# A stage of DeltaNet heads whose order is set by a clock that follows every emitted instruction

## The chip, the cores and the metric

The kernel runs on one core of one Trainium2 chip. The metric is the device time of one execution in microseconds (us); the time before is the median of three runs. Its engines are PE (TensorE, matmul), DVE (VectorE), ACT (ScalarE), POOL (GpSimd) and SP (SyncE, which issues the DMAs here). Each engine executes its own instructions in the order in which the program gives them, and waits at an instruction until the semaphores that it needs have come.

## The reference

One layer of a bidirectional encoder on 1024 tokens and 16 meta tokens, width 1024, float32:

```python
h = rmsnorm(h_res, norm1_w[l])
proj = h @ w_in[l]
(q, k, v, z, b_raw, a_raw, sc_b, sc_c, sc_x, gate_a, gate_b) = jnp.split(proj, SPLIT_POINTS, axis=-1)
o_dn = gated_deltanet_bidir(q, k, v, z, b_raw, a_raw, dn_conv_w[l], A_log[l], dt_bias[l], dn_norm_w[l])
y_a = o_dn @ w_branch_dn[l]
y_b = (sc_b * depthwise_conv_centred(sc_c * sc_x, sc_conv_w[l])) @ w_branch_sc[l]
merged = jax.nn.sigmoid(gate_a) * y_a + jax.nn.sigmoid(gate_b) * y_b
h_res = h_res + merged @ w_out[l]
h2 = rmsnorm(h_res, norm2_w[l])
gu = h2 @ w_gate_up[l]
h_res = h_res + (jax.nn.silu(gu[..., :D_FF]) * gu[..., D_FF:]) @ w_down[l]
```

The DeltaNet has 8 heads of width 128. For each head, q, k and v go through a convolution over five tokens and SiLU; then a gated delta rule runs over chunks of tokens, forwards and backwards. A chunk needs products of keys with keys and of queries with keys times a decay (an exponential of differences of cumulated gates), the inverse of a triangular matrix, and a recurrence with a 128 x 128 state S:

```python
v_new = u_c - jnp.einsum("bhcd,bhde->bhce", w_c, S)
o_c = (jnp.einsum("bhcd,bhde->bhce", qd_c, S)
       + jnp.einsum("bhij,bhje->bhie", qk_c, v_new))
S = S * gl_c[..., None, None] + jnp.einsum("bhcd,bhce->bhde", kd_c, v_new)
```

## The kernel before

Every large product is made of three fp32r matmuls: both operands are split into a high part (a cast on ACT) and a low part (a subtraction on DVE), and high x high, high x low and low x high are summed in a PSUM bank.

The kernel has three stages. In the first 75 us the input is normed, scaled and transposed, and the first units start. In the *stage of heads*, up to about 905 us, PE does two things at once. The *dense units* (`u_qkv`, `u_short`, `u_z`) multiply the whole sequence by 128 columns of `w_in`: the matmuls of L335, in two or three chunks of 320 to 512 tokens with eight steps of three matmuls each. Between two steps the kernel emits what the *streams* have ready. For each head these are: `g_decay` (fetches rows of cumulated gates from DRAM into `PQ`, L507, adds a mask on DVE, L511, and takes the exponential on ACT, L530), `g_norm` (transposes, norms, then for eight chunks the product `kkq` of keys with keys and queries, L587, which DVE multiplies into `NP`, L619, and `PQ`, L625), `g_meta`, `g_inv` (the inverse of eight blocks, with a long chain of small DVE steps in `fs_job`, L477 and L481), `g_vals`, `g_scan` (the recurrence) and `g_out`. The convolutions (L361, with SiLU on ACT at L365) and other chains of DVE are *jobs* in lanes, which `pump` emits where DVE has room. Behind the stage follow the branches, the merge and the feed-forward part, up to 2009 us.

A scan step (`g_scan`) does two directions at a time: S times keys (L807) and queries (L810), r on DVE (L817), `NP` x r (L822), w and v on ACT (L829, L834), keys x w (L839), `PQ` x v (L842), the new S on DVE (L852), and the outputs o (L870, L873, L876).

What is emitted when is planned by the program as it builds the instructions. `T` holds a time for each engine. `pe(ns)` adds to PE's, `on(e, ns)` to another engine's, with flat prices that stand beside each instruction or group; a generator yields the time from which its next step may be emitted, and `run_streams` goes on with it when PE's time has come there. The margins are flat: 200 ns behind PE, 370 behind the others, and 5000 for the decay rows from DRAM:

```python
HOP, TOPE, DEP = 200, 370, 127
ARRIVE = 5000
def on(e, ns, ready=0.0):
    T[e] = max(T[e], ready, T["pe"]) + ns
    return T[e] + TOPE
```

A weight (128 columns) is loaded two units ahead (`pick`), and split in four parts by `split_part`: casts on ACT (L958) and subtractions on DVE (L955), at steps 4, 6, 8 and 10 of the unit before (`SPL`). PSUM has eight banks: three for dense units (`pm`), two for `pe` (transposes, `kkq`), two for `pd` (the scan) and one, `pv`, that values, inverse and outputs share by a lock.

Of the kernel before, what the change touches and what calls it, by code (L numbers as in the profile page):

```python
# [8 lines left out]
F32 = mybir.dt.float32  # L9
# [7 lines left out]
P = 128  # L17
# [17 lines left out]

@with_exitstack
def encoder_layer(ctx: ExitStack, tc: tile.TileContext, x, meta, norm1_w, w_in,
                  dn_conv_w, A_log, dt_bias, dn_norm_w, sc_conv_w, w_bdn, w_bsc,
                  w_out, norm2_w, w_gu, w_down, final_w, out):
    nc = tc.nc  # L40
# [29 lines left out]
    def psv():  # L70
        return ps.tile([P, 512], F32, tag="v", name=uid("pv"), bufs=1)

    rot = {"i": 0}
# [6 lines left out]
    make_identity(nc, ident)  # L80
# [133 lines left out]
    HOP, TOPE, DEP = 200, 370, 127  # L214
    ARRIVE = 5000
    LOAD = 1283
    LAND = 5500
    T = {"pe": 0.0, "dve": 0.0, "act": 0.0, "pool": 0.0}

    def on(e, ns, ready=0.0):  # L220

        T[e] = max(T[e], ready, T["pe"]) + ns
        return T[e] + TOPE

    def pe(ns):
        T["pe"] += ns
        return T["pe"] + HOP

    def V(n, kind=0):
        return on("dve", (68 + 1.042 * n, 130 + 1.042 * n, 130 + 0.52 * n)[kind])  # L230

    def A(n):
        return on("act", 144 + 0.834 * n)
# [40 lines left out]
    def block_sums():  # L274
# [13 lines left out]
        for name, t, terms in (  # L288
# [4 lines left out]
            for k in (slice(0, 2), slice(2, 4)):  # L293
                x0 = terms[0]
                x0 = x0[0](x0[1], k, x0[2]) if isinstance(x0, tuple) else x0[:, k]
                for op, *y in terms[1:]:
                    y = y[0](y[1], k, y[2]) if len(y) == 3 else y[0][:, k]
                    nc.vector.tensor_tensor(out=t[:, k], in0=x0, in1=y, op=op)
                    V(1024)
# [27 lines left out]
    def dense_steps(po, w, xx, t0, n, sweep=False):  # L327
# [6 lines left out]
        for i, (k, j) in enumerate(order):  # L334
            mm(po[:, :n], (wl if j == 2 else wh)[:, k], xl[k][:, t0:t0 + n] if j == 1 else xh[k][:, t0:t0 + n],  # L335
               start=(i == 0), stop=(i == 3 * KT - 1))
            if i % 3 == 2:
                pe(3 * (n / 2.4 + 13))
                yield

# [13 lines left out]
    def conv_job(raw, dst, col, st_, first):  # L354

        for h0, hn in ((first, 520 - first), HALF[1]):
            acc = dst[:, h0:h0 + hn]
            while st_["rows"] < h0 + hn + 4:
                yield max(T["pe"], T["dve"]) + 300
            for t in (0, 1, 3, 4):  # L360
                nc.vector.scalar_tensor_tensor(out=acc, in0=raw[:, h0 + t:h0 + t + hn], scalar=wc[:, t, col:col + 1],  # L361
                                               in1=acc, op0=ALU.mult, op1=ALU.add)
                V(hn, 1)
                yield T["dve"] + DEP
            nc.scalar.activation(acc, acc, AF.Silu)  # L365
            on("act", 0, T["dve"] + HOP)
            t = A(hn)
        yield t

    def u_qkv(h, i, w):  # L370
# [5 lines left out]
        for ci, (t0, n) in enumerate(QUERY if i == 1 else QCH):  # L376
# [14 lines left out]
            nc.scalar.copy(raw[:, 2 + t0:2 + t0 + n], po[:, :n])  # L391
            nc.scalar.activation(dst[:, t0:t0 + n], po[:, :n], AF.Copy, scale=wc[:, 2, col:col + 1])  # L392
            A(n)
            A(n)
            sub["rows"] = 2 + t0 + n if ci < 2 else L + 4
# [9 lines left out]
    def short_job(cx, j, ycs):  # L405
        for i in range(2):
# [3 lines left out]
            yield A(512)  # L410
            for t in range(1, 3):
# [3 lines left out]
                V(512, 1)  # L415
# [3 lines left out]
    def u_short(j, i, w):  # L419
        st_ = shorts[j]  # L420
        if i < 2:
            for t0, n in ((14, 322), (336, 320), (656, 384)):
# [7 lines left out]
                if i == 0:  # L430
                    nc.scalar.copy(sl, po[:, :n])
                    A(n)
                else:
                    nc.vector.tensor_tensor(out=sl, in0=po[:, :n], in1=sl, op=ALU.mult)
                    V(n)
            if i == 1:
                st_["yc"] = []
# [4 lines left out]
        else:  # L442
            force(shorts[-1]["job"])
# [56 lines left out]
    def g_decay(h, st_):  # L500
# [14 lines left out]
        for i0, i1 in ((0, 6), (6, 8)) if h > 1 else ((0, 8),):  # L515
            for i in range(i0, i1):
# [3 lines left out]
                if i - 2 >= i0:  # L520
                    masked(i - 2)
# [1462 lines left out]
```

## Time and profile before

| | |
|---|---|
| runs | 2008.42, 2010.34, 2012.87 us; median 2010.34 |
| profiled execution | 2011.13 us; its span, first to last instruction, 2009.4 us |
| mean granted clock of PE | 0.992 |
| instructions | 32113; matmuls 11914 |
| table loads of ACT | 26, of 1283 ns each |

In the views, a row of a list of instructions gives line, engine, operation, written and read tiles, shape and count; then busy time in us, the mean length in ns, and the idle time of the engine just before, with its releaser. A row of the timeline begins with the start and the length in us (one length for a merged row, "x2"), and gives an idle time before it in brackets. A row of the waits gives who waited for whom, the total in us, how often, and the longest. A row of the windows gives the length of the stretch, then the busy time of each engine with its count of instructions, the granted clock of PE (1.00 is full), the busy share of the DMA engines and GB/s. Small matmuls in full float32 show as two records each.

### The profile page before, as it was taken

What the parts mean: (1) busy time and instruction counts of PE and PEld (TensorE: products, weight loads), DVE (VectorE), ACT (ScalarE), POOL (GpSimd) and SP (SyncE); (2) the same over time, 40 slices, a digit from 0 to 9 for tenths busy, and PEclk for the clock granted to TensorE, in tenths of its full rate; (3) what the DMA queues carried; (4) which work ended last, traced back from release to release, by engine and by line L of the source; (5) the groups of instructions that cost most, each with busy time, mean ns of one, the idle gap of its engine ahead of it and who ended that gap; (6) DMA issues with size and microseconds to landing.
All of it is one profiled execution on the core that took longest, in us unless ns stands there. A gap on an engine that the chain in (4) does not pass through costs nothing.

```text
span 2009.4 us, 32113 instructions
## 1 busy us (share of the span) xinstructions
PE 1951.0 (97%) x11914; PEld 1707.5 (85%) x11914; DVE 1423.4 (71%) x2733; ACT 984.2 (49%) x2198; POOL 164.7 (8%) x497
## 2 busy tenths in 40 slices
PE   9999999899999999999999999999999999999998
PEld 8987889899889989988887788888888888888887
DVE  4757577688768777772666897748887877756574
ACT  5664576767666764631444545224322322225343
POOL 2113200202111120000000000000000000000001
PEclk9999999999999999999999999999999999999999
DMA  4222212122121211244899732322576655487654
GB/s 142 66 59 85 74 49 59 40 60 59 38 60 40 62 46 53 75 159 135 326 307 319 271 128 74 126 92 74 188 241 211 215 168 173 158 283 245 194 177 159
DMA packets 221681, 275.76 MB, mean 137 GB/s; under 512 B 15140, under 2 KB 134341, under 8 KB 220117
## 3 DMA queue, kind: packets, MB, share of 16 engines
q1 hardware_dynamic: 221525, 273.72, 41.8%
q8 instruction: 93, 1.52, 0.3%
q14 instruction: 63, 0.52, 0.1%
HBM read 197.03 MB, written 76.63 MB: 136 GB/s over the span
## 4 chain that ended last, share of the span: by engine, by line
PE 79%; DVE 8%; ACT 7%; DMA 4%; issue 2%; SPq 0%; POOL 0%; POOLq 0%; DVEq 0%; ACTq 0%
PE pm L335 24%; PE pm L1413 4%; PE pm L1710 3%; PE pe L1413 3%; PE pm L1711 3%; PE pm L1709 2%; PE pd L1413 2%; PE pe L1710 2%; PE pd L1710 2%; PE pe L1711 2%; PE pe L1709 2%; PE pd L1709 2%; PE pd L1711 2%; PE pm L1868 1%; PE pm L1867 1%
## 5 line engine op out<-in xcount | busy, mean ns | idle before, releaser
L335 PE MATMUL pm<-hTh,wh 128*128 128x384 f32 (+4 forms) x1200 | 434.2, 363 | 2.1 <-ACT kq L392 1.2
L335 PE MATMUL pm<-al,wh 128*128 128x384 f32 (+4 forms) x1200 | 402.4, 336 | 0.5 <-DVE al L1075 0.5
L335 PE MATMUL pm<-hTh,wl 128*128 128x384 f32 (+4 forms) x1200 | 402.6, 336 | 0.0
L335 PEld LDWEIGHTS pm<-hTh,wh 128*128 128x128 f32 x1200 | 228.0, 190 | 13.2 <-ACT kq L392 1.6
L335 PEld LDWEIGHTS pm<-al,wh 128*128 128x128 f32 x1200 | 228.3, 190 | 9.6 <-DVE al L1075 0.7
L335 PEld LDWEIGHTS pm<-hTh,wl 128*128 128x128 f32 x1200 | 227.3, 190 | 10.2
L89 DVE TENSOR_TENSOR al<-raw,ring_h 128x1024 fp32r<-128x1024 f32 x73 | 88.5, 1222 | 65.2 <-ACT ring_h L88 64.8
L88 ACT CAST ring_h<-raw 128x1024 fp32r<-128x1024 f32 x73 | 76.9, 1055 | 110.9 <-PE pv L1868 37.5
L955 DVE TENSOR_TENSOR wl<-raw,wh 128x512 fp32r<-128x512 f32 x108 | 74.0, 686 | 77.8 <-ACT wh L958 77.6
L361 DVE SCALAR_TENSOR_TENSOR kq<-ra,wc,kq 128x520 f32<-128x520 f32 (+1 forms) x128 | 95.7, 748 | 14.4 <-ACT kq L392 13.0
L88 ACT CAST raw<-pair 128x1024 fp32r<-128x1024 f32 (+1 forms) x56 | 53.8, 961 | 94.9 <-PE pe L1413 31.6
L130 POOL TENSOR_SCALAR ss<-ss 128x1 f32<-128x1 f32 x13 | 4.6, 350 | 1061.1 <-ACT b L1878 602.6
L88 ACT CAST wh<-pair 128x1024 fp32r<-128x1024 f32 (+1 forms) x56 | 53.8, 960 | 59.7 <-PE pv L1413 29.8
L89 DVE TENSOR_TENSOR raw<-pair,raw 128x1024 fp32r<-128x1024 f32 (+1 forms) x56 | 61.9, 1104 | 27.6 <-ACT raw L88 27.5
L89 DVE TENSOR_TENSOR wl<-pair,wh 128x1024 fp32r<-128x1024 f32 (+1 forms) x56 | 61.9, 1105 | 25.1 <-ACT wh L88 25.1
L958 ACT CAST wh<-raw 128x512 fp32r<-128x512 f32 x108 | 66.4, 619 | 23.5 <-PE pm L335 23.3
L829 ACT ACTIVATE w<-pd,small 128x128 f32<-128x128 f32 x128 | 39.9, 364 | 74.2 <-PE pd L822 64.0
L481 DVE TENSOR_TENSOR fP<-fP,tm 128x126 f32<-128x126 f32 (+22 forms) x248 | 62.7, 253 | 6.4
L477 DVE TENSOR_TENSOR tm<-fP,fN 128x126 f32<-128x126 f32 (+22 forms) x248 | 62.6, 253 | 6.2
L132 POOL TENSOR_TENSOR small<-small,minus_half 128x9 f32<-128x9 f32 x16 | 30.6, 1910 | 406.0 <-DVE small L592 255.7
L587 PE MATMUL pe<-kq 128*128 128x256 f32 x128 | 38.7, 403 | 24.3 <-DVE PQ L625 15.1
L1368 DVE TENSOR_TENSOR b<-pm,b 128x512 f32<-128x512 f32 x65 | 43.6, 684 | 24.6 <-PE pm L1711 22.2
(729 smaller groups left out, 5228.5 us busy)
## 6 DMA issues: line engine op xcount, KB each, us to landing
raw<-in_w_in_dram SPq DMA_DIRECT2D x56, 512.0 KB, 4.3
raw<-in_w_gate_up_dram SPq DMA_DIRECT2D x44, 512.0 KB, 5.2
sums<-in_w_down_dram SPq DMA_DIRECT2D x22, 512.0 KB, 4.8
t_d<-sums SPq DMA_DIRECT2D x11, 1024.0 KB, 3.9
raw<-s_d SPq DMA_DIRECT2D x44, 256.0 KB, 3.4
raw<-t_d SPq DMA_DIRECT2D x44, 256.0 KB, 3.7
act_d<-b SPq DMA_DIRECT2D x43, 256.0 KB, 2.7
pair<-in_w_in_dram SPq DMA_DIRECT2D x10, 1024.0 KB, 10.3
```

The source lines that it names most:

```text
L88: nc.scalar.copy(hi, src)
L89: nc.vector.tensor_tensor(out=lo, in0=src, in1=hi.bitcast(F32), op=ALU.subtract)
L335: mm(po[:, :n], (wl if j == 2 else wh)[:, k], xl[k][:, t0:t0 + n] if j == 1 else xh[k][:, t0:t0 + n], start=(i == 0), stop=(i == 3 * KT - 1))
L361: nc.vector.scalar_tensor_tensor(out=acc, in0=raw[:, h0 + t:h0 + t + hn], scalar=wc[:, t, col:col + 1], in1=acc, op0=ALU.mult, op1=ALU.add)
L477: nc.vector.tensor_tensor(out=tv, in0=fP[:, 0:r, j:j + 1].broadcast_to([P, r, n]), in1=fN[:, j:j + 1, j + 1:32].broadcast_to([P, r, n]), o ...
L481: nc.vector.tensor_tensor(out=fP[:, 0:r, j + 1:32], in0=fP[:, 0:r, j + 1:32], in1=tv, op=ALU.subtract)
L955: nc.vector.tensor_tensor(out=u[1][1][:, k], in0=u[2][:, k], in1=u[1][0][:, k].bitcast(F32), op=ALU.subtract)
L958: nc.scalar.copy(u[1][0][:, k], u[2][:, k])
L1413: mm(bank[t], a[:, c], b, start=fresh, stop=first and k == 3 and j == 2, skip_group_check=not first)
L1709: mm(po, ah[:, k], bhk, start=k == 0, stop=False)
L1710: mm(po, ah[:, k], blk, start=False, stop=False)
L1711: mm(po, al[:, k], bhk, start=False, stop=k == 3)
```

## The change

Arithmetic, tiles and instructions stay; 10304 matmuls, 2733 DVE, 1942 ACT, 497 POOL instructions and 852 DMAs are there in both, up to the bank of one tile. Only their order in the stage of heads is another. The change puts a `Clock` behind every call of an engine: it computes when the instruction can start from its own engine's time and from what wrote or read its operands, and takes its price from its kind and size. `V()`, `A()` and `pe()` now only read when the last instruction of that engine ends, plus 25 or 45 ns; `after(x)` says when a tile is ready.

Further: evictions of dense banks are emitted when the clock has the matmuls done (`later`), not right behind them. The exponentials come in groups of six with room between, and a SiLU of a convolution waits until a group is over. A part of a weight is split only once the clock has its input there and the engine free. `kkq` puts two products in one bank and runs up to three ahead. The tile `E` of the inverse lies in `pv` rather than `pm`. In the scan the products with queries come behind L822, both w and v are waited for, and the two additions of an output pair stand together.

```diff
+class Clock:
...
+    def known(self, ap, write=False, e=None):
+        key, p0, p1, lo, hi = self.region(ap)
+        t = self.free.get(key, 0.0) if write else 0.0
+        for r in self.seen[key]:
+            if r[0] < p1 and p0 < r[1] and r[2] < hi and lo < r[3]:
+                t = max(t, 0.0 if e == "pe" == r[6] else r[4], r[5] if write or ap.space == PSUM and e != r[6] else 0.0)
+        return t
...
+    def cost(self, e, op, outs, ins, args):
...
+            if ins[0].dtype == F32R:
+                return m / 2.4 + 14.5, m / 2.4 + 190
...
+            return max(224, m / 0.6 + 9), 212 + max(m, 72) / 0.75
+        if e == "act":
+            t = 150 + 0.79 * n if not psum else 145 + 0.65 * n
...
+    def did(self, e, op, a, kw):
...
+        ready = max([self.known(x, False, e) for x in ins] + [self.known(x, True, e) for x in outs])
+        if e == "sp":
+            start = max(self.T[e], ready + 26)
+            self.T[e] = start + 430
...
+            land = max(start + 1500, self.ring) + n / (20 if run < 64 else 230 if run < 1024 else 330)
+            self.ring = land
+            end = land + 200
+        else:
+            occupied, took = self.cost(e, op, outs, ins, kw)
...
+            start = max(self.T[e], ready + (45 if e == "pe" else 80 if e == "pool" else 34))
...
+    HOP, DEP = 150, 127
+    T = clock.T
+    def on(e):
+        return clock.end[e] + 45
+    def pe():
+        return clock.end["pe"] + 25
+    def after(*aps):
+        return max(clock.known(x) for x in aps) + 45
...
+    def run_late(flush=False):
+        while late and (flush or late[0][0] <= T["pe"]):
+            late.pop(0)[1]()
...
+            while lock["exp"]:
+                yield max(T["pe"], T["dve"]) + 200
             nc.scalar.activation(acc, acc, AF.Silu)
...
-                arrived.append(fetch(i))
-                if i - 2 >= i0:
-                    masked(i - 2)
-            for i in (i1 - 2, i1 - 1):
-                yield arrived[i]
+                yield clock.known(PQ[:, i], True)
+                fetch(i)
+            for i in range(i0, i1):
+                yield after(PQ[:, i])
                 masked(i)
...
+            lock["exp"] = True
...
+                if i % 3 == 2:
+                    yield T["act"] - 300
+            lock["exp"] = False
...
         def kkq(c):
-            pk = psd()
+            if not banks:
+                bank = psd()
+                banks.extend((bank[:, :2 * P], bank[:, 2 * P:]))
+            pk = banks.pop(0)
...
-        E = psm().rearrange("p (d c i) -> p d c i", d=2, c=NC)
+        yield from take("inv")
+        E = psv().rearrange("p (d c i) -> p d c i", d=2, c=NC)
...
-    def split_part(u, i):
+    def split_part(u, i, must=True):
+        k = slice(4 * (i // 2), 4 * (i // 2) + 4)
+        if not must and clock.known(u[1][0][:, k] if i % 2 else u[2]) > max(T["pe"], T[("act", "dve")[i % 2]]):
+            return
...
-            if ahead[0] and n_ in SPL:
-                split_part(ahead[0], SPL.index(n_))
+            run_late()
+            if ahead[0] and n_ >= SPL and ahead[0][3][0] < 4 and n_ % 2 == 0:
+                split_part(ahead[0], ahead[0][3][0], False)
             run_streams()
             pump()
```

Since every call goes through one wrapper, all rows of the changed kernel have its line, L187. Three places show the new order. On ACT, around the first exponentials of the fourth head (`PQ_695`; `wh` is the high part of the next weight, w and v belong to the scan of the second head before it, `ra` and `vT` are evictions), before:

```order
L530 ACT_TABLE_LOAD
L530 ACTIVATE PQ_695<-PQ_695,negG_681 128x128 x12
L958 CAST wh_4314<-raw_4057 128x512
L829 ACTIVATE w_4406<-pd_4373,small_1782 128x128
L829 ACTIVATE w_4408<-pd_4373,small_1782 128x128
L834 ACTIVATE v_673_4410<-pd_4373,small_1782 128x128
L834 ACTIVATE v_674_4412<-pd_4373,small_1782 128x128
L391 COPY ra_4417<-pm_4318 128x336
L392 ACTIVATE vT_3461<-pm_4318,wc 128x336
L958 CAST wh_4314<-raw_4057 128x512
```

And in the changed kernel, at the same exponentials:

```order
L187 CAST wh_3971<-raw_3698 128x512
L187 ACT_TABLE_LOAD
L187 ACTIVATE PQ_695<-PQ_695,negG_681 128x128 x6
L187 ACTIVATE w_4028<-pd_3981,small_1691 128x128
L187 ACTIVATE w_4030<-pd_3981,small_1691 128x128
L187 ACTIVATE v_588_4032<-pd_3981,small_1691 128x128
L187 ACTIVATE v_589_4034<-pd_3981,small_1691 128x128
L187 COPY ra_4042<-pm_3975 128x322
L187 CAST wh_3971<-raw_3698 128x512
L187 ACTIVATE PQ_695<-PQ_695,negG_681 128x128 x6
```

The twelve exponentials have become two sixes, the scan's w and v and the second cast stand between them, and the first cast stands ahead of the table load.

On DVE, at the same place (`wl` is the low part of the weight, which needs the cast; `fP` and `tm` are the inverse of the head before; `NP` is the first product behind `kkq`), before:

```order
L955 TENSOR_TENSOR wl_4315<-raw_4057,wh_4314 128x512
L477 TENSOR_TENSOR tm_4400<-fP_3675,fN_3674 128x70
L481 TENSOR_TENSOR fP_3675<-fP_3675,tm_4400 128x14x5
L477 TENSOR_TENSOR tm_4414<-fP_3675,fN_3674 128x56
L481 TENSOR_TENSOR fP_3675<-fP_3675,tm_4414 128x14x4
L477 TENSOR_TENSOR tm_4427<-fP_3675,fN_3674 128x45
L481 TENSOR_TENSOR fP_3675<-fP_3675,tm_4427 128x15x3
L477 TENSOR_TENSOR tm_4436<-fP_3675,fN_3674 128x30
L955 TENSOR_TENSOR wl_4315<-raw_4057,wh_4314 128x512
L619 SCALAR_TENSOR_TENSOR NP_693<-pe_4379,small_3921,PQ_695 128x128 x2
```

And in the changed kernel, from the masks of the same rows of decay on:

```order
L187 TENSOR_TENSOR PQ_695<-PQ_695,mask_696 128x256 x5
L187 SCALAR_TENSOR_TENSOR r_583_3994<-pd_3981,negEG,vS 128x128
L187 SCALAR_TENSOR_TENSOR r_584_3996<-pd_3981,negEG,vS 128x128
L187 TENSOR_TENSOR PQ_695<-PQ_695,mask_696 128x256
L187 SCALAR_TENSOR_TENSOR kq_3535<-ra_3774,wc,kq_3535 128x520
L187 TENSOR_TENSOR wl_3972<-raw_3698,wh_3971 128x512
L187 SCALAR_TENSOR_TENSOR kq_3535<-ra_3774,wc,kq_3535 128x520
L187 TENSOR_TENSOR fP_3554<-fP_3554,tm_3950 128x5x23
```

The subtraction now stands behind the cast's new place rather than behind all exponentials, the masks are added together and the last one right behind its landing by the clock, and the chain of the inverse is at an earlier point (5x23 against 14x5).

On PE, in the first scan step of the third head, from keys x w to the next S (`w,kn` and `v,PQ` are L839 and L842; `pm` are dense matmuls; `S,kq` is L807), before:

```order
L839 MATMUL pd_4957<-w_4980,kn_2338 128x128
L839 MATMUL pd_4957<-w_4982,kn_2338 128x128
L842 MATMUL pd_4958<-v_744_4984,PQ_694 128x128
L842 MATMUL pd_4958<-v_745_4986,PQ_694 128x128
L335 MATMUL pm_4991<-hTh_137,wh_4613 128x384
L335 MATMUL pm_4991<-al_134,wh_4613 128x384
L335 MATMUL pm_4991<-hTh_137,wl_4614 128x384
L335 MATMUL pm_4991<-hTh_137,wh_4613 128x384
L335 MATMUL pm_4991<-al_134,wh_4613 128x384
L335 MATMUL pm_4991<-hTh_137,wl_4614 128x384
L807 MATMUL pd_5032<-S_5018,kq_1346 128x128
```

And in the changed kernel:

```order
L187 MATMUL pd_4756<-w_4795,kn_2225 128x128
L187 MATMUL pd_4756<-w_4797,kn_2225 128x128
L187 MATMUL pd_4792<-v_714_4799,PQ_694 128x128
L187 MATMUL pd_4792<-v_715_4801,PQ_694 128x128
L187 MATMUL pm_4812<-hTh_137,wh_4427 128x336
L187 MATMUL pm_4812<-al_134,wh_4427 128x336
L187 MATMUL pm_4812<-hTh_137,wl_4428 128x336
L187 MATMUL pd_4835<-S_4825,kq_1384 128x128
```

Three dense matmuls stand between the step's products and the next S where six stood. Over all 56 steps with a next S, the order has six or more dense matmuls there in 54 before and in 7 now; 34 steps have three, and 15 none, with two to four small matmuls in their place.

More of the change, by code (lines that the diff above doesn't have):

```diff
@@ new lines, with __init__, __getattr__, call @@
+class Engine:
+    def __init__(self, engine, name, clock):
+        self.engine, self.name, self.clock = engine, name, clock
+    def __getattr__(self, op):
+        f = getattr(self.engine, op)
+        def call(*a, **kw):
+            r = f(*a, **kw)
+            self.clock.did(self.name, op, a, kw)
+            return r
+        return call
+class Engines:
+    def __init__(self, nc, clock):
+        for field, name in (("tensor", "pe"), ("vector", "dve"), ("scalar", "act"), ("gpsimd", "pool"), ("sync", "sp")):
+            setattr(self, field, Engine(getattr(nc, field), name, clock))
@@ L39, in encoder_layer @@
                   w_out, norm2_w, w_gu, w_down, final_w, out):
-    nc = tc.nc
+    clock = Clock()
+    nc = Engines(tc.nc, clock)
     x, out = x[0], out[0]
@@ L337, in dense_steps, with later @@
             if i % 3 == 2:
-                pe(3 * (n / 2.4 + 13))
+                pe()
                 yield
+    late = []
+    def later(t, f):
+        late.append((t, f))
+        if not rot["later"]:
+            run_late(True)
+    def run_late(flush=False):
+        while late and (flush or late[0][0] <= T["pe"]):
+            late.pop(0)[1]()
     raws = []
@@ L359, in conv_job @@
                 yield max(T["pe"], T["dve"]) + 300
+            yield after(raw[:, h0:h0 + hn + 4], acc)
             for t in (0, 1, 3, 4):
@@ L498, in take @@
         lock["scan"] = who
+        if lock["bank"] is not None:
+            yield clock.known(lock["bank"], True, "pe") + 45
     def g_decay(h, st_):
@@ L605, in g_norm @@
         PQf = PQ.rearrange("p s d t -> p (s d) t")
-        yield T["act"] + HOP - 300
         order = (3, 4, 2, 5, 1, 6, 0, 7)
         ready = lambda c: (c, 0) in st_["exp"] and (c, 1) in st_["exp"]
-        nxt = None
+        ahead_ = []
         for n, c in enumerate(order):
-            while not ready(c):
-                yield T["pe"] + 200
-            pk, t = nxt or kkq(c)
-            nxt = None
-            if n + 1 < NC and ready(order[n + 1]):
-                nxt = kkq(order[n + 1])
-            yield max(t, st_["exp"][c, 0], st_["exp"][c, 1])
+            for c_ in order[n + len(ahead_):n + 3]:
+                while not ready(c_) and not ahead_:
+                    yield T["pe"] + 100
+                if not ready(c_):
+                    break
+                if not banks:
+                    yield after(cc)
+                ahead_.append(kkq(c_))
+            pk, t = ahead_.pop(0)
+            yield max(t, st_["exp"][c, 0], st_["exp"][c, 1], after(cc))
             for d in range(2):
@@ L703, in g_inv @@
         nc.scalar.mul(T2, pt, -1.0)
[L704 removed]
+        yield max(A(), after(W, XT))
         pp, px = (b()[:, :256].rearrange("p (c i) -> p c i", c=NC) for b in (psv, psm))
```

387 lines of the change are left out of this document (237 added, 150 removed).

## The prediction

> **What bounds the kernel now.** I read the page first, then the windows by stage, the list of waits of each engine, and the timeline around the longest waits.
>
> ```profile
> span 2009.4 us, 32113 instructions
> PE 1951.0 (97%) x11914; PEld 1707.5 (85%) x11914; DVE 1423.4 (71%) x2733; ACT 984.2 (49%) x2198; POOL 164.7 (8%) x497
> PE 79%; DVE 8%; ACT 7%; DMA 4%; issue 2%; SPq 0%; POOL 0%; POOLq 0%; DVEq 0%; ACTq 0%
> ```
>
> TensorE (PE) is busy for 97% of the span, and it is 79% of the chain that ended last. Its work does not change: the change issues the same instructions on each engine. So a gain can only be time in which PE waits, or runs below its clock. The order of the two kernels is the same at the start and again in the long feed-forward part, so the second question is how much of this lies in the stage of heads, which runs from about 75 us to 905 us.
>
> ```profile
> core 0: us, PE busy (x) PEld busy (x) DVE busy (x) ACT busy (x) POOL busy (x), PEclk, DMA share, GB/s
> 75.00:905.00 830.00, 790.85 (x6605) 742.09 (x6605) 605.35 (x1668) 530.61 (x1578) 128.97 (x409) 0.98 0.22 65
> 905.00:2009.40 1104.40, 1091.40 (x4862) 901.20 (x4860) 776.98 (x978) 413.47 (x538) 16.43 (x34) 1.00 0.57 194
> ```
>
> PE idles 830.0 - 790.9 = 39.2 us in the stage of heads, and its granted clock there is 0.98, not 1.00. VectorE (DVE) is 73% busy and ScalarE (ACT) 64%: neither is full. These are the waits of PE in that window (total, times, longest):
>
> ```profile
> PE pe L587 <- DVE PQ L625: 15.1, 9, 2.9
> PE pe L587 <- DVE fP L481: 9.2, 3, 3.6
> PE pd L822 <- DVE r L817: 4.6, 2, 2.7
> PE pd L807 <- DVE S L852: 1.4, 2, 0.7
> PE pd L839 <- ACT v L834: 1.4, 3, 0.6
> ```
>
> L587 is the product of keys with keys and queries; it waits for one of two PSUM banks, which DVE frees with L625. Its two rows are 24.3 us, well over half of the idle time. Why is DVE late? The wait list of DVE and the timeline of the longest case say it:
>
> ```profile
> DVE wl L955 <- ACT wh L958: 69.0, 29, 10.9
> ```
>
> ```profile
> 355.20 1.28 ACT L530 ACT_TABLE_LOAD   x1
> 356.49 3.62 ACT L530 ACTIVATE PQ<-PQ,negG 128x128 f32<-128x128 f32 x12
> 360.02 0.60 ACT L958 CAST wh<-raw 128x512 fp32r<-128x512 f32 x1
> 360.66 0.69 DVE L955 TENSOR_TENSOR wl<-raw,wh 128x512 fp32r<-128x512 f32 x1 [4.66 <-ACT wh L958]
> 364.38 0.41 DVE L625 TENSOR_TENSOR PQ<-pe,PQ 128x256 f32<-128x256 f32 x1
> 364.94 0.87 PE L587 MATMUL pe<-kq 128*128 128x256 f32 x2 [3.63 <-DVE fP L481]
> 365.93 0.53 PE L335 MATMUL pm<-al,wh 128*128 128x384 f32 x1
> ```
>
> The cast L958, the first half of splitting a weight, stands on ACT behind a table load and twelve exponentials. The second half L955 was put on DVE at a fixed step, so DVE, which is in order, stands still for 4.66 us with everything behind it, L625 too, and PE then waits 3.63 us. The last row shows the second price: the dense matmul is on the array for 0.53 us, and this window shows why:
>
> ```profile
> 365.00:370.00 5.00, 4.57 (x18) 4.14 (x18) 4.45 (x14) 1.38 (x7) 2.73 (x11) 0.66 0.08 19
> ```
>
> The granted clock is 0.66 in the 5 us behind the wait. The Trainium skill, page "TensorE: Matmul & The Clock Gate", section "Why this matters for your kernels", says that the array keeps its full rate if no gap between bursts is over about 3 us. The trace agrees for this gap of 3.63 us, and no sum below goes by it.
>
> **The change part by part.** The sum is made against the profiled execution: 2011.13 us, of which 2009.4 are the span. The median of the runs is 2010.34, 0.8 lower.
>
> *Weights split on landing, exponentials in sixes, the clock.* In the first fence of order the cast L958 has moved ahead of the exponentials or between the two sixes, and on DVE (second fence) its partner is emitted only when the clock has the cast done. So the chain "table load, twelve exponentials, cast, subtraction, product" no longer holds DVE. The new product code also puts two products in a bank, so four may be outstanding where two were. Of the 24.3 us I count 20 as gone; at worst, with only the longest cases cured, 12.
>
> *The clock of the array.* 0.02 x 830 = 16.6 us of clock were not granted (12.5 to 20.8 by the rounding of 0.98), some of it while PE was idle anyway. Half-rate stretches follow long waits, so they go with them: 11, between 5 and 17.
>
> *The other visible waits.* 39.2 - 24.3 = 14.9 us lie in many short waits of the scan, the inverse and the weights. The clock prices each hand-over where the old one used a flat 200 or 370 ns. I count half of them, 8 (4 to 13).
>
> *Waits that no idle time shows.* In this stretch a dense matmul takes 0.32 us, but the next starts 0.15 later, so a wait under about 0.16 us is not seen as idle.
>
> ```profile
> 500.90 0.32 PE L335 MATMUL pm<-al,wh 128*128 128x322 f32 x1
> 501.05 0.31 PE L335 MATMUL pm<-hTh,wl 128*128 128x322 f32 x1
> 501.20 0.60 PE L839 MATMUL pd<-w,kn 128*128 128x128 f32 x4
> 501.65 0.61 PE L842 MATMUL pd<-v,PQ 128*128 128x128 f32 x4
> 501.92 0.60 DVE L852 SCALAR_TENSOR_TENSOR S<-S,eGl,pd 128x128 f32<-128x128 f32 x2 [0.43 <-PE pd L839]
> 502.01 0.39 PE L335 MATMUL pm<-hTh,wh 128*128 128x322 f32 x1
> ```
>
> PE has some 400 rows in the stage that wait for DVE or ACT, so the ceiling is 64 us and the floor 0. The visible waits of the scan rows above are few, so I stay near the floor: 10 (0 to 30). Sum of the gains: 20 + 11 + 8 + 10 = 49.
>
> *What it costs: the state's hand-over.* Each of 56 scan steps hands the state S from PE to DVE and back. By the rows above S needs 502.52 - 501.20 = 1.32 us from the first L839. In that time PE has L839 and L842 (0.81 us, from 501.20 to 502.01) and then dense matmuls at 0.15. Before, six to nine stood there in nearly all steps (third fence): 1.7 to 2.2 us, a cushion. Now, by the order, 34 steps have three (1.26), 15 have only two to four small matmuls (taken as two thirds of three dense ones: 0.81 + 0.30 = 1.11), 7 have six or more. With DVE free the shortfall is 34 x 0.06 + 15 x 0.21 = 5 us; a DVE instruction that stands ahead of S now adds its time to PE, and behind the waiting matmul all dense work is queued. I take 6, between 2 and 17 (56 x 0.30, half of the L852 row).
>
> *The masks.* The decay rows come from DRAM, and DVE adds the mask when they have landed. The old code allowed 5000 ns; the new clock computes 1500 + 285 + 200 + 45 = 2030 ns from the issue.
>
> ```profile
> PQ<-grow SPq DMA_DIRECT2D x128, 64.0 KB, 3.0
> DMA to landing us min/median/max: 2.8/3.0/4.6
> DVE PQ L511 <- DMA PQ<-grow: 1.6, 3, 0.6
> ```
>
> The landing takes 3.0 us at the median and never under 2.8, so each last mask can hold DVE for about 1.0 us: 6 heads x 3 masks that are put down right after their landing = 18 us of DVE against 1.6 now. Behind them stand convolution steps with slack, and sometimes S or r. I take a fifth on the path, 4 (0 to 18).
>
> *Table loads.* Sixes with other work between them raise the loads, as the order of ACT lists them, from 26 to 32.
>
> ```profile
> L530 ACT ACT_TABLE_LOAD x9 | 11.5, 1283 | 0.2
> L530 ACT ACTIVATE PQ<-PQ,negG 128x128 f32<-128x128 f32 x128 | 39.0, 388 | 0.1
> ```
>
> 6 x 1.283 = 7.7 us of ACT, covered by its 299 idle us in the stage; on the path they would cost 7.7. I take 0. The Trainium skill, page "ScalarE: Activation LUTs", section "What ACT_TABLE_LOAD costs", says that a drain of about 1.38 us goes with each switch; by it the six would be an estimated 16 us. The trace disagrees: the exponentials start at 356.49, right behind a load of 1.28 that began at 355.20.
>
> *Late evictions*, the order within the scan (second products after L822, additions in pairs) and the other bank for the inverse move instructions and add none; their worth is in the terms above, their price 0, since DVE and ACT are off the path by the window's shares. One doubt stays: the clock prices an exponential at 251 ns, the trace at (3.62 - 0.39) / 11 = 294. It runs early by that much, and so I left part of each gain uncounted.
>
> Sum: 49 - 6 - 4 = 39. 2011.1 - 39 = 1972; as a median, 1971.
>
> **The rivals.**
>
> *It all goes.* Then 24.3 + 16.6 + 14.9 + 16 of hidden waits come back less 4 of hand-over: 68, so 1942 by the median. For it: there is dense work to put in every gap, and DVE is idle for 225 us of the stage. Against it: the clock is 17% short for an exponential and about 1 us for a landing, so some waits stay.
>
> *The wait only moves.* In the bursts ACT itself may be the bound:
>
> ```profile
> 545.00:550.00 5.00, 2.67 (x19) 2.41 (x17) 2.52 (x9) 4.86 (x14) 0.95 (x3) 0.96 0.00 0
> 560.00:565.00 5.00, 5.00 (x121) 4.60 (x120) 2.58 (x5) 4.89 (x15) 2.67 (x11) 1.00 0.01 3
> ```
>
> ACT is 97% busy here, and none of its work goes away. Then PE would wait at the scan or the inverse for what it no longer waits for at L587, and only a fourth of the 49 comes: 12, so 1998. Against it: the second row shows a full ACT beside a full PE, and over the whole stage ACT is 64% busy.
>
> *Slower: no cushion at the hand-overs.* The new clock hands work over with 25 to 45 ns to spare, where the old one kept 200 to 370. If DVE is really later than the clock has it (masks, cheaper prices), PE stalls at every S and every r (56 + 64 = 120 hand-overs in the scan), with no other matmul allowed past. It breaks even at 49 / 120 = 0.41 us each, more than one L852; at 0.6 us it costs 72 - 49 = 23 us: 2033. For it: the masks' 1.0 us. Against it: most hand-overs have nothing long ahead of them in the new order of DVE, and a stall gives DVE time to catch up.
>
> *No change.* That the change does not do what it says is ruled out by the order, in the three fences. Terms that cancel to within 0.2% (4 us, about what a measurement of this kernel can tell from none) are left.
>
> **How the numbers follow.** Forecast (a gain of 20 to 60): 0.60, 1971 us. It all goes: 0.13, 1942. The wait only moves: 0.12, 1998. Slower: 0.10, 2033. Within 4 us: 0.05. With all terms at their worst the gains are 12 + 5 + 4 + 0 = 21 and the costs 17 + 18 = 35, a loss of 14; at their best 24 + 17 + 13 + 30 = 84 less 2, a gain of 82. I leave out half of the first rival and most of the last two: 1944 to 2004. Faster 0.60 + 0.13 + 0.12 = 0.85, less 0.01 for the thin end of the moved wait: 0.84; same 0.05; slower 0.11.
>
> **What would show it right or wrong.** Right: in the stage of heads the idle time of PE falls from 39 us to 10 to 20, and the stage ends near 866 us; the products wait under 6 us in total; DVE's wait for the cast falls from 69 us to under 25; the granted clock is 0.99 or 1.00; the part behind the stage keeps its 1104 us. The masks' wait for the DMA should rise from 1.6 us to 8 or more, and S at the scan should be the largest wait of PE that is left. Wrong: idle time of PE over 30 us, wherever its releaser now is; or a stage that is no shorter though the idle time has gone, which would mean short waits at the hand-overs, to be seen as wider starts of the scan's matmuls; or a later stage that grew.

## The result and the profile after

The changed kernel takes 1984.55 us (median of 4 runs, 1983.66 to 1988.73) against 2011.38 for the kernel before (4 runs): a ratio of 0.9873, 95% interval [0.9854, 0.9891]. About 27 us came where 39 were forecast. Its profiled execution took 1984.57 us. The page, and the windows by stage with the later boundary moved to the new end of the stage of heads:

```profile
span 1982.9 us, 32162 instructions
PE 1949.6 (98%) x11914; PEld 1697.7 (86%) x11914; DVE 1413.5 (71%) x2733; ACT 989.4 (50%) x2204; POOL 168.4 (8%) x497
PE 83%; DVE 8%; DMA 4%; issue 1%; ACT 1%; POOL 1%; SPq 0%; POOLq 0%; DVEq 0%; ACTq 0%
```

```profile
75.00:878.00 803.00, 789.86 (x6610) 732.39 (x6611) 595.87 (x1669) 539.34 (x1595) 133.48 (x409) 1.00 0.23 67
878.00:1982.90 1104.90, 1091.83 (x4862) 902.18 (x4860) 776.97 (x978) 410.06 (x528) 15.62 (x33) 1.00 0.58 193
```

The whole gain is in the stage of heads: it ends at 878 instead of 905, and what follows takes 1104.9 us against 1104.4. PE's idle time there went from 39.2 to 803.00 - 789.86 = 13.1 us, and the granted clock from 0.98 to 1.00. One thing does not fit: idle time fell by 26 and the clock should have given back some 10 more, yet the stage is 27 shorter. PE's busy time, 789.86 against 790.85, should have fallen with the clock and did not. The waits of PE in the stage (who waited for whom, total, times, longest):

```profile
PE pe L187 <- DVE Nm L187: 7.0, 4, 4.6
PE pe L187 <- issue: 2.9, 1, 2.9
PE pm L187 <- ACT kq L187: 1.9, 1, 1.9
PE pe L187 <- DVE PQ L187: 1.4, 5, 0.4
PE pd L187 <- DVE S L187: 0.6, 2, 0.4
```

The two rows of the products, 24.3 us before, are 1.4 (`PQ`). The largest wait is one that nothing in the forecast spoke of: `Nm`, 4.6 us of it in one piece. The timeline shows that place:

```profile
146.18 0.18 POOL L187 TENSOR_TENSOR meta_inv<-meta_inv,tm 16x1 f32<-16x1 f32 x1
146.30 0.17 POOL L187 MEMSET small<- 128x99 f32 x1
146.50 0.27 ACT L187 ACTIVATE jk<-pe 16x128 f32<-16x128 f32 x1 [4.91 <-POOL small L187]
146.90 0.16 DVE L187 TENSOR_TENSOR Nm<-pe,Dm 16x16 f32<-16x16 f32 x1 [4.58 <-ACT jk L187]
147.11 1.11 PE L187 MATMUL pe<-ident,kq 128*128 128x128 f32 x4 [4.64 <-DVE Nm L187]
```

ACT, DVE and PE all stand for 4.6 to 4.9 us behind a memset of 0.17 us, because on POOL that memset was queued behind the chain of small steps of `g_meta`. A half-rate stretch of PE follows: the granted clock is 0.51 from 146.8 to 150.3.

Where the rest went shows in the waits of the *weight loads* (PEld). A matmul's own row hides a wait that the matmul before it covers; the load before it shows it. The three rows of the scan on r, v and S, before:

```profile
PEld pd L822 <- DVE r L817: 5.3, 2, 3.2
PEld pd L839 <- ACT v L834: 3.8, 11, 0.9
PEld pd L807 <- DVE S L852: 1.9, 2, 1.0
```

and after:

```profile
PEld pd L187 <- ACT v L187: 6.2, 22, 0.7
PEld pd L187 <- DVE r L187: 3.7, 10, 0.8
PEld pd L187 <- DVE S L187: 3.5, 12, 0.7
```

A few long waits have become many short ones: 15 with 11.0 us before, 44 with 13.4 us after. One of them in the timeline:

```profile
688.25 0.61 ACT L187 ACTIVATE v<-pd,small 128x128 f32<-128x128 f32 x2
688.50 0.31 PE L187 MATMUL pm<-hTh,wl 128*128 128x320 f32 x1
688.91 0.52 PEld L187 LDWEIGHTS pd<-w,kn 128*128 128x128 f32 x4 [0.36 <-ACT v L187]
688.91 0.71 PE L187 MATMUL pd<-w,kn 128*128 128x128 f32 x4
```

The dense matmul at 688.50 leaves the next start free 0.15 us later, at 688.65. The load waits until 688.91, by its releaser for ACT's v, and PE's row has no bracket: 0.26 us are lost with no idle time shown.

To size it I compared starts: for each matmul in the stage, the time since the start of the one before, less the lower quartile of the same succession of three shapes in the whole trace of before. Summed over the stage, in us (number of places in brackets; places outside the half-rate stretches but for the first and last row):

| excess of a start | before | after |
|---|---|---|
| over 0.6 us, everywhere | 41.5 (26) | 10.9 (7) |
| 0.05 to 0.6 us | 18.9 (166) | 33.7 (279) |
| under 0.05 us | 21.8 | 24.5 |
| half-rate stretches, without waits over 0.6 | 14.0 | 3.1 |

The difference is 30.6 + 10.9 - 14.8 - 2.7 = 24 us of the stage's 27. So the long waits and the clock did come back, 41.5 us of them, and 17.5 went into short waits. The second row depends on the choice of the quartile's sample: with other choices it rises by 10 to 15 us. Two thirds of its rise lie in three groups of the scan: the starts of keys x w, S x keys and `NP` x r hold 16.5 us at 136 places after, 6.8 at 53 before.

### The profile page after: what moved, and what is told of

It reads as the page before. It is cut to its first block, busy times and chain, and to the rows that moved or that the text cites. A ratio compares the mean times of both kernels' runs of the same rounds, so it can differ in the third digit from the quotient of the medians.

```text
span 1982.9 us, 32162 instructions
## 1 busy us (share of the span) xinstructions
PE 1949.6 (98%) x11914; PEld 1697.7 (86%) x11914; DVE 1413.5 (71%) x2733; ACT 989.4 (50%) x2204; POOL 168.4 (8%) x497
## 4 chain that ended last, share of the span: by engine, by line
PE 83%; DVE 8%; DMA 4%; issue 1%; ACT 1%; POOL 1%; SPq 0%; POOLq 0%; DVEq 0%; ACTq 0%
PE pm L187 45%; PE pd L187 18%; PE pe L187 13%; PE pv L187 8%; DMA o_d<-w 1%; DMA w<-o_d 1%; DVE kq L187 1%; DMA PQ<-grow 1%; DVE NP L187 1%; DVE PQ L187 1%; DVE wl L187 1%; DMA pair<-p_d 1%; DVE pair L187 1%; DVE al L187 1%; DVE vT L187 0%
## 5 line engine op out<-in xcount | busy, mean ns | idle before, releaser
L187 PE MATMUL pm<-hTh,wh 128*128 128x384 f32 (+4 forms) x1234 | 442.1, 359 | 1.9 <-ACT kq L187 1.9
L187 PE MATMUL pm<-al,wh 128*128 128x384 f32 (+4 forms) x1234 | 414.0, 336 | 0.5 <-DVE al L187 0.5
L187 PE MATMUL pm<-hTh,wl 128*128 128x384 f32 (+4 forms) x1234 | 413.4, 336 | 0.0
L187 PEld LDWEIGHTS pm<-hTh,wh 128*128 128x128 f32 x1234 | 233.5, 189 | 13.8 <-ACT kq L187 2.1
L187 PEld LDWEIGHTS pm<-al,wh 128*128 128x128 f32 x1234 | 233.6, 189 | 10.8 <-DVE al L187 0.7
L187 PEld LDWEIGHTS pm<-hTh,wl 128*128 128x128 f32 x1234 | 232.2, 188 | 11.1
L187 DVE TENSOR_TENSOR al<-raw,ring_h 128x1024 fp32r<-128x1024 f32 x73 | 88.4, 1223 | 63.8 <-ACT ring_h L187 63.3
L187 ACT CAST ring_h<-raw 128x1024 fp32r<-128x1024 f32 x73 | 76.9, 1054 | 110.1 <-PE pv L187 33.8
L187 ACT CAST wh<-raw 128x512 fp32r<-128x512 f32 (+1 forms) x134 | 93.6, 703 | 74.1 <-PE pm L187 36.1
L187 DVE TENSOR_TENSOR wl<-raw,wh 128x512 fp32r<-128x512 f32 (+1 forms) x132 | 102.9, 780 | 33.6 <-ACT wh L187 33.1
L187 ACT CAST raw<-pair 128x1024 fp32r<-128x1024 f32 (+1 forms) x56 | 53.8, 961 | 94.4 <-PE pe L187 31.6
L187 DVE SCALAR_TENSOR_TENSOR kq<-ra,wc,kq 128x520 f32<-128x520 f32 (+1 forms) x128 | 95.9, 750 | 3.3 <-ACT kq L187 1.8
L187 POOL TENSOR_SCALAR ss<-ss 128x1 f32<-128x1 f32 x13 | 4.6, 352 | 1072.8 <-ACT b L187 602.8
L187 ACT CAST wh<-pair 128x1024 fp32r<-128x1024 f32 (+1 forms) x56 | 53.8, 960 | 59.5 <-PE pv L187 29.8
L187 DVE TENSOR_TENSOR raw<-pair,raw 128x1024 fp32r<-128x1024 f32 (+1 forms) x56 | 61.9, 1106 | 29.0 <-ACT raw L187 28.9
L187 DVE TENSOR_TENSOR wl<-pair,wh 128x1024 fp32r<-128x1024 f32 (+1 forms) x56 | 62.0, 1107 | 24.8 <-ACT wh L187 24.8
L187 PE MATMUL pd<-S,kq 128*128 128x128 f32 x480 | 77.9, 282 | 0.7 <-DVE S L187 0.6
L187 PEld LDWEIGHTS pd<-S,kq 128*128 128x128 f32 x480 | 64.5, 191 | 7.6 <-DVE S L187 3.5
L187 ACT ACTIVATE w<-pd,small 128x128 f32<-128x128 f32 x128 | 39.9, 363 | 61.6 <-PE pd L187 50.3
L187 DVE TENSOR_TENSOR tm<-fP,fN 128x126 f32<-128x126 f32 (+22 forms) x248 | 62.8, 253 | 5.9
L187 DVE TENSOR_TENSOR fP<-fP,tm 128x126 f32<-128x126 f32 (+22 forms) x248 | 62.8, 253 | 5.9
L187 POOL TENSOR_TENSOR small<-small,minus_half 128x9 f32<-128x9 f32 x16 | 29.6, 1848 | 398.8 <-DVE small L187 398.8
```

The lines of the kernel that those rows point to most:

```text
L187: r = f(*a, **kw)
```

## The experiments

Two theories. **Hand-overs**: the clock's prices are short by some 50 ns and it hands over with 25 to 45 ns to spare, so PE reaches many operands a little early. **Blocked queues**: the rest is lost at few places, where an engine stands whole microseconds (the memset on POOL, the masks behind their landing). The prices on which the first rests, as groups of the changed kernel in the stage (busy us, mean ns):

```profile
L187 DVE SCALAR_TENSOR_TENSOR S<-S,eGl,pd 128x128 f32<-128x128 f32 x104 | 31.9, 344 | 40.8 <-PE pd L187 34.0 <-ACT PQ L187 3.3 <-ACT wh L187 1.2
L187 ACT ACTIVATE PQ<-PQ,negG 128x128 f32<-128x128 f32 x128 | 40.2, 396 | 0.3 <-DVE PQ L187 0.2
L187 ACT ACTIVATE v<-pd,small 128x128 f32<-128x128 f32 x128 | 40.1, 372 | 0.0
```

The clock has 76 + 1.03 x 128 + 83 = 291 ns for S, 150 + 0.79 x 128 + 105 = 356 for the exponential and 145 + 0.65 x 128 + 105 = 333 for v: 53, 40 and 39 ns short.

All experiments had the kernel before on the same chip, four kernels to a group. Its medians were 2012.67, 2012.63 and 2013.22 us in the three groups, and the ratios below are to it. Between experiments I compare ratios, times 2012.6.

**The changed kernel itself (c0_after).** No edit.

> The changed kernel itself, on the chip of the three runs beside it, as their measure. Both theories expect 1984 to 1986 us and a ratio of 0.986 to 0.988. Theory of the hand-overs: what is missing from the forecast (27 us came, 39 were forecast) is lost in very many waits of 0.05 to 0.2 us in the scan, because the clock hands over with no margin. Theory of the blocked queues (rival): it is lost at a few places where an engine stands for whole microseconds behind an instruction that the clock priced too low (a memset of POOL behind the chain of the meta block, 4.9 us; masks that wait for DMAs, 12 us of DVE in total).

1985.59 us, ratio 0.9862 [0.9846, 0.9879]. This is the base of all that follows but one. In rows of the runs below, L189 or L191 is the wrapper's line where an edit has added lines.

**A margin at every hand-over (e1_margin).**

```diff
-        return clock.end[e] + 45
+        return clock.end[e] + 245
-        return clock.end["pe"] + 25
+        return clock.end["pe"] + 175
...
                 while not job.done:
+                    lock["exp"] = False
```

The last line lifts the pause of the convolutions, for a convolution that is forced while it pauses.

> The changed kernel with 200 ns more margin behind DVE and ACT and 150 ns more behind PE (245 and 175 ns in place of 45 and 25). Theory of the hand-overs: most of the short waits go, PE's busy time in the stage of heads falls by 8 us or more at the same work, and the time falls by 6 to 14 us, to 1971 to 1979. Theory of the blocked queues: 150 or 200 ns change nothing about waits of microseconds; within 3 us of 1984.6.

1968.71 us, ratio 0.9781 [0.9765, 0.9797]: 16 us faster, a larger gain than the hand-overs' range had. PE's busy time in the stage falls from 790.8 us to 779.2 (in c0_after, 75 to 878 us, and here, 75 to 863), as that theory said.

**All prices as the traces show them (e2_prices).**

```diff
-            t = 150 + 0.79 * n if not psum else 145 + 0.65 * n
+            t = 210 + 0.643 * n if not psum else 145 + 0.65 * n
+            if psum and hasattr(args.get("scale"), "tensor"):
+                t = 150 + 0.83 * n
...
+            elif op == "scalar_tensor_tensor":
+                t = 124 + 1.046 * n
...
-            end = land + 200
+            end = land + (1150 if run < 1024 else 200)
```

> The changed kernel with prices of the clock set to the trace: exponentials and other ACT operations from SBUF 210 + 0.643 n, ACT with a scale per partition from PSUM 150 + 0.83 n, scalar_tensor_tensor of DVE 124 + 1.046 n, the landing of small DMAs 950 ns later. Theory of the hand-overs: short waits fall by a third, 3 to 6 us, to 1979 to 1982, less than the margin gives. Theory of the blocked queues: DVE's wait for the masks' DMA falls from 12 us to under 3, and the time by 3 to 6 us, but the POOL place stays; 1979 to 1982. The two part by where the gain lies: at many scan rows, or at the masks.

1957.70 us, ratio 0.9727 [0.9712, 0.9741]: 27 us faster than the changed kernel, as much again as the whole change had brought. Both theories had this far too low. The place at the memset did not stay, as the second theory had it, but went, though no price of POOL was touched. From 75 to 850 us, PE now idles 1.9 us (775.00 - 773.07):

```profile
75.00:850.00 775.00, 773.07 (x6575) 729.58 (x6575) 584.92 (x1642) 526.76 (x1561) 129.05 (x408) 1.00 0.23 67
```

**The memset on DVE (e5_memset).**

```diff
-        nc.gpsimd.memset(small, 1.0)
+        nc.vector.memset(small, 1.0)
```

> The changed kernel with the memset of the tile small on DVE instead of POOL, where it stood 4.9 us behind the chain of the meta block while ACT, DVE and PE waited. Theory of the hand-overs: that place is 2 to 3 us at most, since the dense work lost there is done elsewhere; 1982 to 1984. Theory of the blocked queues: the 4.6 us of PE and the half-rate stretch of 3.4 us behind it (1.7 us) go, 5 to 7 us; 1978 to 1980.

1980.20 us, ratio 0.9837 [0.9821, 0.9853]: 5 us, what the blocked queues gave this place. In its timeline the three engines stand there for under 0.9 us each:

```profile
143.95 0.27 ACT L187 ACTIVATE jk<-pe 16x128 f32<-16x128 f32 x1 [0.89 <-DVE small L187]
144.34 0.16 DVE L187 TENSOR_TENSOR Nm<-pe,Dm 16x16 f32<-16x16 f32 x1 [0.42 <-ACT jk L187]
144.55 0.42 PEld L187 LDWEIGHTS pe<-ident,kq 128*128 128x128 f32 x4 [0.36 <-DVE Nm L187]
```

The intervals of e5_memset and c0_after overlap, so the size rests on the timeline: the 4.6 us of wait and the half-rate stretch behind it are gone. Against that, the half-rate stretch at the start of the stage is longer in this trace, 6.8 us from 74.6 where c0_after has 3.4 from 75.3.

**Which price it was (p1_landing, p2_dve, p3_act).** Each has one part of e2_prices: the landing (last line of its diff), scalar_tensor_tensor on DVE, the two prices of ACT. They, and the other variants of the changed kernel below but the last, keep the pause for every job but a forced convolution (no run has this edit alone):

```diff
-            while lock["exp"]:
+            while lock["exp"] and not lock.get("forced"):
```

> The changed kernel, with the clock's landing of DMAs with rows under 1024 bytes put 950 ns later, as the traces show it; no other price is touched. All prices together had brought 28 us of the changed kernel's 1985.6. Theory of the landing: the masks that DVE waits for (12 us in the trace of the changed kernel) hold up all that stands behind them on DVE, so this one price is most of it: 16 to 24 us, 1962 to 1970. Theory of the hand-overs: the masks have slack behind them, and the many short waits come from the prices of DVE and ACT: 3 to 7 us here, 1979 to 1983. Both: DVE's wait for the landing falls from 12 us to under 3.

> The changed kernel, with scalar_tensor_tensor on DVE priced as the trace shows it (about 50 ns more for 128 and for 520 columns), and no other price touched. Theory of the hand-overs: S, r, NP and the convolution's steps are of this kind, so each short wait behind them shrinks: 8 to 15 us, 1971 to 1978. Theory of the landing: at most 4 us, 1982 to 1987.

> The changed kernel, with ACT's exponentials and scaled copies from SBUF at 0.29 us for 128 columns where the clock had 0.25, and its scaled evictions from PSUM 60 to 90 ns longer, and no other price touched. Theory of the hand-overs: w, v, the casts behind the exponentials and the evictions are met better: 6 to 12 us, 1974 to 1980. Theory of the landing: at most 4 us, 1982 to 1987.

Landing: 1981.27 us, ratio 0.9845 [0.9822, 0.9868], 3 us. DVE: 1967.84 us, 0.9781 [0.9758, 0.9805], 16 us. ACT: 1971.82 us, 0.9801 [0.9774, 0.9827], 12 us. The intervals of p1_landing and c0_after overlap. The sum, 32, is more than the 27 of all together, because one thing is counted in each: the wait of PE at the memset, in the rows of `Nm`, 6.8 us in c0_after, is 1.9, 1.2 and 0.4 in the three runs and 0.2 in e2_prices. Each of these edits moves the whole order, and the place went with it. The count of late starts keeps the two apart (us in the stage):

| excess of a start | c0_after | p1_landing | p2_dve | p3_act | e2_prices |
|---|---|---|---|---|---|
| over 0.6 us, and half-rate stretches | 13 | 7 | 6 | 5 | 3 |
| 0.05 to 0.6 us | 33 | 36 | 23 | 27 | 18 |

So the theory of the hand-overs holds for the larger part: some 10 us of DVE's gain, 6 of ACT's and 15 of all prices' are short late starts. The rest, 8 to 10 us in ACT's run and with all prices, is long waits and half rate at few places, as the theory of the blocked queues would count them; how much of that the prices cured, and how much went by luck of the new order, is not separated. The landing brings nothing to the short starts, although DVE's wait for it did go. First the changed kernel's row, then that of p1_landing:

```profile
DVE PQ L187 <- DMA PQ<-grow: 12.2, 14, 2.3
```

```profile
DVE PQ L187 <- DMA PQ<-grow: 2.1, 3, 1.2
```

DVE got 10 us back, and the time fell by no more than the place at the memset explains. The waits of the scan's weight loads say it crosswise. With DVE's price (p2_dve):

```profile
PEld pd L189 <- ACT v L189: 5.3, 18, 0.8
PEld pd L189 <- DVE r L189: 0.8, 3, 0.3
PEld pd L189 <- DVE S L189: 0.4, 1, 0.4
```

With ACT's prices (p3_act):

```profile
PEld pd L189 <- DVE S L189: 5.0, 11, 1.2
PEld pd L189 <- DVE r L189: 2.7, 12, 0.4
PEld pd L189 <- ACT v L189: 1.0, 5, 0.3
```

DVE's price takes away the waits for what DVE makes (r and S, 22 to 4) and leaves those for ACT's v; ACT's prices do the reverse (v, 22 to 5). With all of them (e2_prices) four waits are left of 44, and starts late by 0.05 to 0.6 us are 166 with 18.5 us, as many as before the change.

**The margin alone (e1b_margin).** e1_margin with the pause held as in the three kernels above.

> The margins of the run before (200 ns more behind ACT, DVE and POOL, 150 more behind PE) on the changed kernel, but with the pause of the convolutions during the exponentials lifted only for a convolution that is forced, which leaves the changed kernel's own order as it is. That run lifted the pause at every forced job, so its gain of 17 us could be in part from that. If the margin did it: 1965 to 1972 again. If the lifted pause did it: 1980 to 1986.

1968.00 us, ratio 0.9783 [0.9759, 0.9807]: the wider lift of the pause had done nothing that can be measured, so the gain is the margin's. Here too the place at the memset is gone: the row of `Nm` is 1.5 us, and 1.3 in e1_margin.

**Prices, memset and half the margin (q_pm100).** e2_prices and e5_memset together, with `+ 145` and `+ 105` where the changed kernel has 45 and 25.

> The changed kernel with all three groups of measured prices (ACT, DVE, landing), the memset of small on DVE, and margins 100 ns larger behind ACT, DVE and POOL and 80 ns behind PE. Theory of the hand-overs: prices and margin cure the same short waits, so the margin adds little to what the prices bring: 1948 to 1957, at most 10 us below the 1957.7 of the prices alone. If they cure different waits, the gains add (28 + 5 + 9): 1940 to 1946. If a margin behind correct prices only keeps ready work back: 1958 to 1966.

1964.39 us, ratio 0.9761 [0.9744, 0.9778]: slower than the prices alone. By its number the third case, but the reason I gave for that, ready work kept back everywhere, is not what the trace shows. Late starts are fewer still (152 with 16.5 us); the time is lost at one place:

```profile
810.47 0.50 PE L191 MATMUL pm<-hTh,wh 128*128 128x512 f32 x1 [3.09 <-ACT wh L191]
813.14 0.69 DVE L191 TENSOR_TENSOR rb<-pm,rb 128x512 f32<-128x512 f32 x1 [3.29 <-DMA rb<-yc_d]
814.49 0.80 PE L191 MATMUL pm<-hTh,wl 128*128 128x512 f32 x1 [3.28 <-DVE wl L191]
```

The split of a weight came too late. PE waits for the cast, then DVE stands 3.29 us for a DMA with the subtraction behind it, and PE waits again. A half-rate stretch of 6.8 us goes with them. So little was left to cure, for the margin at the short waits as the first theory has it, and for the memset too, whose place was gone in e2_prices. Against e2_prices this run has three edits, the margin, the memset and the pause of a forced convolution; which of them moved the split behind a blocked queue is not separated, and whether a margin without this place would gain anything was not tried.

**The split alone, on the kernel before (b1_split_only).**

```diff
-            A(512)
+            u[3][1:] = [A(512)]
...
-            if ahead[0] and n_ in SPL:
-                split_part(ahead[0], SPL.index(n_))
+            if ahead[0] and n_ >= 4 and ahead[0][3][0] < 4 and n_ % 2 == 0 and (
+                    ahead[0][3][0] % 2 == 0 or ahead[0][3][1] <= T["pe"]):
+                split_part(ahead[0], ahead[0][3][0])
```

> The kernel before, where only the subtraction of a weight's part waits, by the old planner's own time, for the cast to be done. If the cast that DVE stood waiting for is what made PE wait for its products (the account of the forecast), the 24 us of L587's waits fall to under 10 and DVE's 69 us for the cast in the stage to under 30: 1992 to 2003. If those waits came from the old clock's flat prices and its two banks of one product each, DVE stands less for the cast but L587's waits stay over 15 us: 2004 to 2013. The split's new places also make the order of ACT switch tables 8 times more (34 against 26), at most 10 us.

2002.55 us, ratio 0.9951 [0.9937, 0.9965]: 10 us faster than before. Waits of PE in its stage, then DVE's for the cast:

```profile
PE pv L698 <- ACT vS L765: 10.5, 3, 4.3
PE pv L698 <- DVE W L683: 4.4, 4, 2.4
PE pd L839 <- ACT v L834: 3.4, 1, 3.4
PE pv L85 <- ACT o L914: 3.0, 2, 2.0
PE pe L587 <- DVE PQ L625: 3.0, 5, 0.8
```

```profile
DVE wl L955 <- ACT wh L958: 19.8, 9, 7.3
```

The forecast's account of the cause holds: once the cast no longer holds DVE, L587's waits fall from 24.3 to 3.0. But under the old planner other waits grow in their place, those of the inverse and the outputs (L698, L85) and of v, and 10 us net remain of 21.

**One product in a bank (e7_one_bank).** In `kkq` each product has a bank of its own again, and two are outstanding.

```diff
-                banks.extend((bank[:, :2 * P], bank[:, 2 * P:]))
+                banks.append(bank[:, :2 * P])
...
-            for c_ in order[n + len(ahead_):n + 3]:
+            for c_ in order[n + len(ahead_):n + 2]:
```

> The changed kernel with one product of keys in a bank and two outstanding, as before the change, and all else as it is. If the bank of two products cured the waits of L587, they come back: 10 to 20 us more than the changed kernel's 1985.6, so 1995 to 2006. If the split and the clock did, the bank has nothing left to do: 1981 to 1990.

1992.99 us, ratio 0.9903 [0.9889, 0.9918]: 8 us slower than the changed kernel, between the two cases. The visible wait of the products is small:

```profile
PE pe L187 <- DVE PQ L187: 3.9, 9, 1.8
```

It was 1.4 us. More late starts hold some 3 to 5 of the 8 us, by the choice of the quartile's sample (0.05 to 0.6 us: 295 with 37.7 us against 276 with 32.9 in c0_after). The half-rate stretch at the memset is 6.8 us long here and was 3.4. The rest was not followed.

**Twelve exponentials in one piece (e4_twelve_exps).**

```diff
-                if i % 3 == 2:
-                    yield T["act"] - 300
```

> The changed kernel with the twelve exponentials of a group in one piece again, so 26 table loads in place of 32. If the pause between the sixes was needed for w, v and the casts, PE waits behind the exponentials again: 4 to 12 us more, 1989 to 1997. If the clock meets them by placing the work elsewhere, the six loads saved (7.7 us of ACT, covered) change nothing: 1981 to 1989.

1982.02 us, ratio 0.9850 [0.9834, 0.9867], whose interval overlaps that of c0_after: the sixes bring nothing that can be measured, and their six table loads cost nothing that can be.

## Why the prediction was right, and where it was not

1971 was forecast, in a range of 1944 to 2004; 1984.55 came. The mechanism was right and one term had the wrong sign. The range, wide as it was, held that error of some 20 us too.

*Long waits: right.* 20 for the products and 8 for the others were counted; starts late by over 0.6 us fell by 30.6. The cause that was named, the cast that holds DVE, is shown by b1_split_only. Not every credit given to a part held: the split alone gains 10 net, the bank of two products 8, the sixes nothing that can be measured.

*The clock of the array: right.* 11 counted; the half-rate stretches cost 14.0 - 3.1 = 10.9 us less.

*Waits that no idle time shows: wrong, and this is the step that failed.* "The visible waits of the scan rows above are few, so I stay near the floor: 10" took a gain for granted, and the state's hand-over was priced apart at 6. Together they were a gain of 4; starts late by less than 0.6 us cost 14.8 + 2.7 = 17.5 us more than before. The forecast had the doubt in hand, that the clock's exponential is 251 ns and the trace's 294, and let it pass as "part of each gain uncounted". It never set the other prices beside their rows. DVE's was the dearer one, 53 ns on S and as much on r and each convolution step; the two experiments gained 16 us with it and 12 with ACT's, of which some 10 and 6 are short waits.

*The state's hand-over: right place, too narrow.* The cushion behind S was counted and the one before r, w and v was not: of the 44 waits 12 are for S, 10 for r and 22 for v. That S would be the largest visible wait left was wrong: 0.6 us, against 7.0 for `Nm`, whose longest, 4.6, goes back to a queue (POOL) that the sum did not look at; the run without it was 5 us faster, with intervals that overlap.

*The masks: right for DVE, not shown for the time.* DVE's wait rose from 1.6 to 12.2 us, as told. The 4 us that were taken for it on the path are not seen: the price that takes the wait away gains 3, within the intervals, and in the same run the place at the memset goes.

*Table loads: right.* Six more, nothing measurable.

*Signs.* Idle time 13.1 (10 to 20 forecast), products 1.4 (under 6), clock 1.00, the later part 1104.9: as told. The stage ended at 878 and not near 866, for the short waits. DVE's wait for the cast in the stage fell from 69.0 us, but not quite to under 25:

```profile
DVE wl L187 <- ACT wh L187: 27.6, 11, 5.7
```

*The rivals.* "It all goes" failed in part for a reason given against it, the short price of the exponential; the landing, the other reason, is not seen in the time, and DVE's price was not named. 27 us more came once the prices were the trace's: 1957.7, most of the way to its 1942. "No cushion at the hand-overs" had the right mechanism, and missed the size: some 0.3 us at 44 places, not 0.6 at 120.

*What stays open.* Late evictions alone, the split back at fixed steps, and the order within the scan were not tried by themselves. The split's 10 us were measured on the kernel before and the bank's 8 on the changed one, so what the clock's placing brought of the 27 as a whole is not separated. POOL's prices were left as they are: the clock takes 0.31 us for each tensor_scalar in the chain of `g_meta`, and the trace has the first of them at 0.95. And since each edit of a price moves the whole order, and a place such as that of the memset comes and goes with it, gains of 5 us or less (p1_landing, e4_twelve_exps) can't be put down to the price or the group by their size alone.

## What to carry over

A planner that follows each instruction is only as good as its prices: before it hands work over with 45 ns to spare, set every price beside the mean of its row, since with 40 to 53 ns too little on its main kinds of instruction the changed kernel was 27 us slower than with measured prices, as much as the planner had gained. Look for short waits in the rows of the weight loads and in the starts of the matmuls, because PE's idle time does not show them. And follow each small instruction on a seldom-used queue: a 0.17 us memset there held three engines for 4.6 us.

## What the runs showed of the hardware

A wait of PE shorter than 3 us can be followed by half rate. In the kernel before, a wait of 2.18 us at 567.7 to 569.87 stood in a window of full clock, and the next 3.4 us had 0.51 (the wait in the timeline, then the windows, whose column ahead of the last two is the granted clock):

```profile
569.87 0.99 PE L587 MATMUL pe<-kq 128*128 128x256 f32 x2 [2.18 <-DVE PQ L625]
```

```profile
565.00:570.00 5.00, 2.82 (x19) 2.59 (x18) 3.33 (x7) 4.91 (x9) 0.00 (x0) 1.00 0.14 52
570.00:573.40 3.40, 3.40 (x26) 2.90 (x28) 3.40 (x9) 0.00 (x0) 0.00 (x0) 0.51 0.19 36
```

The Trainium skill, page "TensorE: Matmul & The Clock Gate", section "Why this matters for your kernels", which the prediction cited for gaps over about 3 us, is not contradicted by the long gaps (3.63 us before and 4.64 after, each with a half-rate stretch behind it); by this row a shorter one can cost the same.

A full-float32 matmul whose operand is waited for costs more than the wait. In the scan of the changed kernel the second matmul of such a pair mostly started 0.21 us after the first (in 58 of 63 pairs whose first was over 0.02 us late), where undisturbed pairs are 0.11 apart. So a wait of 0.1 us counts about twice, by an estimate from these two numbers.
